# Linear attention on one core: where the middle pairs' K features lie, and who makes the last group's V blocks

## The chip, the cores and the metric

The kernel runs on one core of one Trainium2 chip. The metric is the device time of one execution in microseconds (us). A core has five engines that run their own instruction streams in order: TensorE (PE, with its weight loads PEld), VectorE (DVE), ScalarE (ACT), GpSimd (POOL) and SyncE (SP). They wait for each other by semaphores. 16 DMA engines move data between the main memory and the on-chip buffers; a transfer is issued by an engine, here by POOL (queue q0) or by SP (queue q1).

## The reference

Q, K and V have the shape 8 x 12 x 512 x 64 (batch, heads, positions, features), in float32. Features are `max(0, x) + 1`. For each of the 96 heads a 64 x 64 matrix of keys and values is made, and a sum of the K features; each query row is then multiplied with both and divided.

```python
Q_feat = np.maximum(0, Q) + 1
K_feat = np.maximum(0, K) + 1
KV = np.einsum('bhkd,bhkv->bhdv', K_feat, V)
K_sum = np.sum(K_feat, axis=2)
numerator = np.einsum('bhqd,bhdv->bhqv', Q_feat, KV)
denominator = np.einsum('bhqd,bhd->bhq', Q_feat, K_sum)
return numerator / (denominator[:, :, :, None] + 1e-10)
```

## The kernel before

The 96 heads are cut into 12 groups of 8 heads, and these into 6 pairs of groups (pair s holds groups 2s and 2s + 1). Everything is issued in an order written out by hand. `load_pair` loads V, K and Q of a pair from POOL, narrowing them to bf16 on the way, two pairs ahead. The first half of Q is loaded by SP into a tile of the pool that later holds the output (`load_first_q`).

For a group, `k_features` (VectorE, L180) makes the K features, and `v_blocks` makes four copies of V, each multiplied with one of four 0/1 masks of partitions (`v_all`). Two of the blocks are made in full by ScalarE (L213); of the other two VectorE makes all (L211): in the code `cut = 2 if b < 2 else 0`, where `cut` says how many of a block's two halves VectorE makes. `sums` (POOL, L200) puts the masks beside V, so that the same matmuls give the sum of the K features. `keys_values` (TensorE, L237, L246 or L256) adds up features times V blocks over 16 steps in PSUM; it is called in quarters. `keys_values_copies` (ScalarE, L271) copies the result to `kva_all`. `q_features` (VectorE, L180), `transposes` (TensorE, L284) and `transpose_copies` (ScalarE, L289) prepare Q. `output` makes, for each of four parts (g, h, i) of a group, the out matmuls (L302) into one of two PSUM tiles, and then `norms`: a reciprocal (L318) and a multiply (L319) on VectorE, which writes to the output tile `o_sb`. The out matmuls of the third part need the PSUM tile that the norms of the first part free. `output` takes a list `between`, whose first two entries are called after the first and the second norms.

Iteration s makes the output of pair s - 1 and the keys and values of pair s. The last one (s = 5, `end`) has an order of its own: K features and VectorE's V blocks of the last group, 11, stand at its start, ahead of `output(8)`.

K features lie in two tiles `kf_all` of 8 KB a partition. The first and the last pair (`WIDE`) use a layout with zeros beside the features, one tile for each group. The middle pairs need no zeros, and share the first tile in two halves (`kf_halves`). Before the last pair's group 11 can use that tile, POOL clears its zeros again (`clear`, L98), after iteration 4.

The pool of output tiles has five buffers (`OUT_BUFS`). Seven tiles are taken from it in turn: the first load of Q, and the outputs of pairs 0 to 5. A tile that comes to a used buffer waits for the last use of it, for an output the landing of its two stores. `store` issues a group's store: groups 0 to 9 from POOL (L164), groups 0 to 5 after iteration 3, 6 and 7 after iteration 4, 8 and 9 after iteration 5; group 10 in one and group 11 in five pieces from SP (L169 to L177).

Of the kernel before, what the change touches and what calls it, by code (L numbers as in the profile page):

```python
# [8 lines left out]
FP32 = mybir.dt.float32  # L9
BF16 = mybir.dt.bfloat16  # L10
# [9 lines left out]
def kernel(  # L20
# [16 lines left out]
    nc = tc.nc  # L37

    B, H, S, D = Q.shape
    P = 128  # L40
    C = 8
# [4 lines left out]
    NP = 4  # L46
    NG = NPAIR // NP
# [4 lines left out]
    def view(t, c):  # L52
# [15 lines left out]
    out_pool = ctx.enter_context(tc.tile_pool(name="out_pool", bufs=OUT_BUFS))  # L68
# [11 lines left out]
    kva_diag = [kva_all[:, i] for i in range(NV)]  # L80


    WIDE = (0, NG // 2 - 1)
    SHORT = NG // 2 - 2
    kf_all = [wide.tile([P, C2, 2, 2, D], BF16, name=f"kf_all_{i}") for i in range(2)]
    kf_halves = kf_all[0].rearrange("p c n h d -> p (c n h d)").rearrange(
        "p (i c n d) -> p i c n d", i=2, n=2, d=D
    )

    def kf_of(g):  # L90
        if g // 2 == 0:
            return kf_all[g]
        return kf_all[1 - g % 2] if g // 2 in WIDE else kf_halves[:, g % 2]

    def clear(t, engine):
        for h in range(2):
            zeros = t[64 - 64 * h : P - 64 * h].rearrange("p c n h d -> p (c n) h d")[:, :, h]
            engine.memset(zeros.bitcast(FP32), 0.0)  # L98
# [12 lines left out]
    def load_first_q():  # L111
        t = out_pool.tile([P, 2 * NP, C, D], FP32, name="o_sb")
        half = t[:, 0:NP].rearrange("p n c d -> p (n c) d")
        nc.sync.dma_start(out=half, in_=q_eights[:, 0])
        return half

    def load_rest_q(t):
        u = in_pool.tile([P, 2, C4, D], BF16, name="q_raw")
# [65 lines left out]
    def k_features(g):  # L184
        k_raw = raw.pop(("k", g))
        kf = kf_of(g)
        for n in range(2):
            if g // 2 in WIDE:
                for h in range(2):
                    ps = slice(64 * h, 64 * h + 64)  # L190
                    feature(kf[ps, :, n, h], k_raw[ps, n])
            else:
                feature(kf[:, :, n], k_raw[:, n])

    def mask_of(g):
        return mask_short if g // 2 == SHORT else mask
# [7 lines left out]
    def v_blocks(g, engine):  # L204
        v_raw = raw["v", g]
        mask = mask_of(g)
        for b in range(4):
            block = v_all[:, g % 2, :, :, b, 0:D]
            cut = 2 if b < 2 else 0
            if engine == "dve" and cut > 0:  # L210
                nc.vector.tensor_scalar_mul(block[:, 0:cut], v_raw[:, 0:cut], mask[:, b : b + 1])  # L211
            if engine == "act" and cut < 2:
                nc.scalar.mul(out=block[:, cut:], in_=v_raw[:, cut:], mul=mask[:, b : b + 1])  # L213
# [10 lines left out]

    def keys_values(g, lo=0, hi=C2):
        kf = kf_of(g)
        if g % 2 == 0 and lo == 0:
            kva_ps[g // 2] = [psum_kva.tile([P, BANK], FP32, name="kva_ps") for _ in range(2)]
        halves = kva_ps[g // 2]
        for c in range(lo, hi):  # L230
            for n in range(2):
                if g < 2:
                    eight, first, last_c = g, (c, n) == (0, 0), (c, n) == (C2 - 1, 1)
                else:
                    eight, first, last_c = n, g % 2 == 0 and c == 0, g % 2 == 1 and c == C2 - 1
                if g // 2 in WIDE:
                    nc.tensor.matmul(  # L237
                        halves[eight][:, 0 : 4 * DV],
                        lhsT=kf[:, c, n],
                        rhs=v_all[:, g % 2, n, c],  # L240
                        start=first,
                        stop=last_c,
                    )
                    continue
                if g // 2 == SHORT:
                    nc.tensor.matmul(  # L246
                        halves[g % 2][64 * n : 64 * n + 64, 0 : 4 * DV],
                        lhsT=kf[:, c, n],
                        rhs=v_all[:, g % 2, n, c],
                        start=c == 0,  # L250
                        stop=c == C2 - 1,
                    )
                    continue
                for h in range(2):
                    ps = slice(64 * h, 64 * h + 64)
                    nc.tensor.matmul(  # L256
                        halves[h][64 * eight : 64 * eight + 64, 0 : 4 * DV],
                        lhsT=kf[ps, c, n],
                        rhs=v_all[ps, g % 2, n, c],
                        start=first,  # L260
                        stop=last_c,
                    )
# [65 lines left out]
    def output(g, between=()):  # L328

        cells = [(g, h, i) for h in range(2) for i in range(2)]  # L330
        for k in range(4):
            if k >= 2:
                norms(*cells[k - 2])
                if k - 2 < len(between):
                    between[k - 2]()
            out_matmuls(*cells[k])
        norms(*cells[2])
        norms(*cells[3])

    def iteration(s):  # L340


        a, b = 2 * s, 2 * s + 1
        end = b == NG - 1
        quarter = C2 // 4

        def turned(g):
            transposes(g)
            transpose_copies(g)

        def first_half():
            turned(a)
            if not end:
                turned(b)
            keys_values(b, 0, quarter)

        def second_half():
            if end:
                turned(b)
            keys_values(b, quarter, 2 * quarter)  # L360

        if end:
            k_features(b)
            v_blocks(b, "dve")
        v_blocks(b, "act")
        output(a - 2, [lambda lo=lo: keys_values(a, lo, lo + quarter) for lo in (0, quarter)])
        keys_values(a, 2 * quarter, C2)
        q_features(a)
        q_features(b)
        if not end:  # L370
            k_features(b)
            v_blocks(b, "dve")
        output(a - 1, (first_half, second_half))
        keys_values(b, 2 * quarter, C2)
        if not end:
            v_blocks(a + 2, "act")
        keys_values_copies(s)
        if not end:
            k_features(a + 2)
            v_blocks(a + 2, "dve")  # L380
# [5 lines left out]

    with tc.manual_schedule():
        q_first = load_first_q()
        load("k", (0,))
        load("v", (0,))  # L390
        load_rest_q(q_first)
        load("k", (1,))
        load("v", (1,))
        for t in kf_all:
            clear(t, nc.vector)
        make_identity(nc, identity)
        nc.vector.tensor_reduce(
            out=mask,
            in_=identity.rearrange("p (h b x) -> p b h x", h=2, b=4),
            op=ALU.add,  # L400
            axis=mybir.AxisListType.XY,
        )
        nc.vector.tensor_reduce(
            out=mask_short,
            in_=identity.rearrange("p (b x) -> p b x", b=4),
            op=ALU.add,
            axis=mybir.AxisListType.X,
        )
        for i in range(2):
            t = v_all[:, i].rearrange("p n c b x -> p (n c) b x")  # L410
            nc.vector.memset(t[:, :, :, D1:], 0.0)
            sums(i, nc.vector)
        for t in kva_diag:
            for b in range(4):
                nc.gpsimd.memset(t[:, b], 0.0)
        load_pair(1)
        blocks(0)
        keys_values(0)
        q_features(0)
        q_features(1)  # L420
        transposes(0)
        blocks(1)
        transpose_copies(0)
        transposes(1)
        transpose_copies(1)
        keys_values(1)
        load_pair(2)
        keys_values_copies(0)
        blocks(2)
        for s in range(1, NG // 2):  # L430
            iteration(s)
            if s == SHORT - 1:
                sums(2 * SHORT, nc.gpsimd)
            if s + 2 < NG // 2:
                load_pair(s + 2)
            if s == SHORT - 1:
                sums(2 * SHORT + 1, nc.gpsimd)
            if s == SHORT:
                sums(2 * SHORT + 2, nc.gpsimd)
                clear(kf_all[0], nc.gpsimd)  # L440
                sums(2 * SHORT + 3, nc.gpsimd)
            for g in range(2 * s - 2, 2 * s) if s > 3 else range(2 * s) if s == 3 else ():
                store(g)
        output(NG - 2)
        output(NG - 1)
        for g in range(NG - 2, NG):
            store(g)
# [30 lines left out]
```

## Time and profile before

| | |
|---|---|
| time, median of 3 runs | 125.47 us (125.41 to 125.51) |
| the profiled execution | 125.6 us, span 123.8 us |
| granted TensorE clock, mean | 0.89 |
| DVE busy | 91.4 us (74%) |
| PE busy | 70.3 us (57%) |
| ACT busy | 69.0 us (56%) |
| POOL busy | 31.2 us (25%) |
| DMA queue q0 (POOL) | 28.84 MB, 95.1% of 16 engines' span |
| DMA queue q1 (SP) | 3.15 MB, 6.7% |

The span runs from the first to the last instruction in the profile; the execution's own time has some 1.8 us around it. Busy time of an engine is the time in which it has an instruction running. "Idle before" and the name after an arrow tell how long the engine sat without work ahead of an instruction, and what ended that. `x4` counts instructions merged into one line. A line's L number is that of the kernel before; in the changed kernel the same lines stand two to five further down.

### The profile page before, as it was taken

How to read it: one execution, taken by the hardware profiler on the slowest of the kernel's cores; microseconds unless marked ns; L12 is line 12 of the kernel's file. 1: busy time of each engine (PE TensorE's matmuls, PEld its weight loads, DVE VectorE, ACT ScalarE, POOL GpSimd, SP SyncE). 2: the span in 40 equal slices, each digit the busy share in tenths (PEclk: the TensorE clock that was granted, in tenths of full speed). 3: DMA queues.
4: the chain of work that ended last, by engine and by line, in shares of the span. 5: the costliest groups of instructions: out<-in, count | busy, mean ns of one | idle time of the engine just before them, and what ended most of it. 6: DMA issues, size and time to landing. Idle time of an engine off the chain costs nothing.

```text
span 123.8 us, 2524 instructions
## 1 busy us (share of the span) xinstructions
PE 70.3 (57%) x1056; PEld 52.6 (42%) x1056; DVE 91.4 (74%) x186; ACT 69.0 (56%) x73; POOL 31.2 (25%) x58
## 2 busy tenths in 40 slices
PE   0000099881596758676667746969214999944300
PEld 0000068661375436454455625957111578732200
DVE  5788771009179999998999969899799589449700
ACT  0006939729964999499945999179990003340000
POOL 6990000600000510024030673213912043020000
PEclk9999999999679999999999998699955589998555
DMA  3999999999999999999999999999999999999993
GB/s 98 335 213 213 213 213 214 216 216 213 214 214 216 212 214 213 217 216 213 211 209 212 215 219 212 218 212 213 216 314 417 419 419 421 417 408 418 406 406 130
DMA packets 9412, 32.15 MB, mean 260 GB/s; under 512 B 568, under 2 KB 824, under 8 KB 9272
## 3 DMA queue, kind: packets, MB, share of 16 engines
q0 software_dynamic: 8032, 28.84, 95.1%
q1 hardware_dynamic: 1368, 3.15, 6.7%
q8 instruction: 8, 0.13, 0.4%
q14 instruction: 4, 0.03, 0.1%
HBM read 37.75 MB, written 12.58 MB: 406 GB/s over the span
## 4 chain that ended last, share of the span: by engine, by line
DMA 38%; DVE 20%; PE 19%; ACT 10%; POOL 3%; issue 3%; ACTq 0%; POOLq 0%
DMA k_raw<-in_K_dram 27%; DMA v_raw<-in_V_dram 11%; PE kva_ps L237 9%; DVE o_sb L319 8%; ACT v_all L213 6%; PE qt_ps L284 5%; DVE kf_all L180 5%; DVE v_all L211 3%; PE o_ps L302 3%; ACT qt L289 3%; DVE qf L180 3%; PE kva_ps L256 2%; DVE recip L318 2%; POOL v_raw L137 1%; ACT kva_all L271 1%
## 5 line engine op out<-in xcount | busy, mean ns | idle before, releaser
L213 ACT ACTIVATE v_all<-v_raw,mask 128x2048 bf16<-128x2048 bf16 x24 | 46.6, 1994 | 2.4 <-DMA v_raw<-in_V_dram 2.1
L319 DVE TENSOR_TENSOR o_sb<-o_ps,recip 128x512 f32<-128x512 f32 x48 | 33.2, 692 | 1.6
L237 PE MATMUL kva_ps<-v_all,kf_all 128*128 128x272 bf16 x128 | 19.7, 316 | 19.3 <-ACT v_all L213 15.7
L302 PE MATMUL o_ps<-kva_all,qt 128*64 128x130 bf16 x384 | 19.8, 238 | 12.3 <-ACT kva_all L271 6.1
L289 ACT COPY qt<-qt_ps 128x512 f32<-128x512 f32 x24 | 12.9, 588 | 23.0 <-PE qt_ps L284 23.0
L237 PEld LDWEIGHTS <-kf_all 128*128 128x128 bf16 x128 | 13.6, 109 | 23.5 <-DVE v_all L211 15.7
L302 PEld LDWEIGHTS <-qt 128*64 128x64 bf16 x384 | 14.4, 118 | 20.6 <-issue 9.4
L180 DVE TENSOR_SCALAR kf_all<-k_raw 64x1024 bf16<-64x1024 bf16 (+1 forms) x32 | 14.6, 477 | 11.5 <-DMA k_raw<-in_K_dram 11.2
L256 PE MATMUL kva_ps<-v_all,kf_all 64*64 64x272 bf16 x384 | 15.5, 292 | 7.4 <-ACT v_all L213 4.1
L211 DVE TENSOR_SCALAR v_all<-v_raw,mask 128x2048 bf16<-128x2048 bf16 x24 | 17.2, 759 | 1.1 <-DMA v_raw<-in_V_dram 1.1
L318 DVE RECIPROCAL recip<-o_ps 128x8 f32<-128x8 f32 x48 | 9.6, 199 | 8.8 <-PE o_ps L302 8.7
L284 PE MATMUL qt_ps<-identity,qf 128*128 128x128 f32 x96 | 13.3, 281 | 4.4 <-DVE qf L180 2.8
L180 DVE TENSOR_SCALAR qf<-q_raw 128x1024 bf16<-128x1024 bf16 x22 | 15.1, 761 | 0.4 <-DMA q_raw<-in_Q_dram 0.4
L164 POOL DMA_DIRECT2D out_dram<-o_sb x10 | 9.6, 961 | 21.7 <-DVE o_sb L319 12.0
L256 PEld LDWEIGHTS <-kf_all 64*64 64x64 bf16 x384 | 10.4, 110 | 9.5 <-issue 5.2
L284 PEld LDWEIGHTS qt_ps<-identity,qf 128*128 128x128 f32 x96 | 10.2, 140 | 6.8 <-DVE qf L180 3.5
L271 ACT CAST kva_all<-kva_ps 64x260 bf16<-64x260 f32 x24 | 8.9, 372 | 5.6 <-PE kva_ps L237 5.3
L137 POOL DMA_DIRECT2D v_raw<-in_V_dram x4 | 2.9, 735 | 34.6 <-ACT qt L289 21.9
L246 PE MATMUL kva_ps<-v_all,kf_all 128*64 128x272 bf16 x64 | 6.3, 339 | 2.2 <-DVE v_all L211 2.2
L213 ACT ACT_TABLE_LOAD x1 | 1.3, 1283 | 10.4 <-DMA v_raw<-in_V_dram 10.4
L246 PEld LDWEIGHTS <-kf_all 128*64 128x64 bf16 x64 | 4.6, 135 | 2.6 <-DVE v_all L211 2.6
L200 POOL CAST v_all<-mask 128x128 bf16<-128x128 f32 x4 | 3.7, 916 | 7.2 <-DVE o_sb L319 6.5
(21 smaller groups left out, 24.3 us busy)
## 6 DMA issues: line engine op xcount, KB each, us to landing
out_dram<-o_sb POOLq DMA_DIRECT2D x10, 1024.0 KB, 24.0
v_raw<-in_V_dram POOLq DMA_DIRECT2D x5, 1024.0 KB, 13.6
k_raw<-in_K_dram POOLq DMA_DIRECT2D x5, 1024.0 KB, 17.8
q_raw<-in_Q_dram POOLq DMA_DIRECT2D x5, 1024.0 KB, 21.9
o_sb<-in_Q_dram SPq DMA_DIRECT2D x1, 1024.0 KB, 4.8
k_raw<-in_K_dram POOLq DMA_DIRECT2D x2, 512.0 KB, 9.5
v_raw<-in_V_dram POOLq DMA_DIRECT2D x2, 512.0 KB, 11.3
out_dram<-o_sb SPq DMA_DIRECT2D x1, 1024.0 KB, 6.9
```

The lines of the kernel that those rows point to most:

```text
L180: nc.vector.tensor_scalar(out=dst, in0=src, scalar1=1.0, scalar2=1.0, op0=ALU.add, op1=ALU.max)
L211: nc.vector.tensor_scalar_mul(block[:, 0:cut], v_raw[:, 0:cut], mask[:, b : b + 1])
L213: nc.scalar.mul(out=block[:, cut:], in_=v_raw[:, cut:], mul=mask[:, b : b + 1])
L237: nc.tensor.matmul(halves[eight][:, 0 : 4 * DV], lhsT=kf[:, c, n], rhs=v_all[:, g % 2, n, c], start=first, stop=last_c,)
L246: nc.tensor.matmul(halves[g % 2][64 * n : 64 * n + 64, 0 : 4 * DV], lhsT=kf[:, c, n], rhs=v_all[:, g % 2, n, c], start=c == 0, stop=c == C ...
L256: nc.tensor.matmul(halves[h][64 * eight : 64 * eight + 64, 0 : 4 * DV], lhsT=kf[ps, c, n], rhs=v_all[ps, g % 2, n, c], start=first, stop=l ...
L271: nc.scalar.copy(out=kva[ps, :, n, :], in_=halves[tile_][at, 0 : 4 * DV].rearrange("p (b x) -> p b x", b=4)[:, :, 0:D1],)
L284: nc.tensor.transpose(qt_ps[g][half][:, r], qf[:, r, half], identity)
L289: nc.scalar.copy(out=to[:, g % 2 * 2 + half].rearrange("p (q r) -> p q r", r=R), in_=t.rearrange("p r q -> p q r"),)
L302: nc.tensor.matmul(o_ps[64 * j : 64 * j + 64, c // 2 % 2, (c % 2) * W : (c % 2) * W + W], lhsT=qt[:, c // 2, q : q + 16, :, c % 2], rhs=kv ...
L318: nc.vector.reciprocal(out=recip, in_=cells[:, :, :, :, D:D1])
L319: nc.vector.tensor_tensor(out=outs[g // 2][:, 2 * h + g % 2 : 2 * NP : NP, 4 * i : 4 * i + 4].rearrange("p n (b c) d -> p b c n d", b=2), ...
```

## The change

Three things. The middle pairs' K features no longer lie in the first `kf_all` tile but in a tile taken from the output pool right after the first load of Q (`place_kf_halves`), so that eight tiles go through its five buffers; both `kf_all` tiles keep their zeros, and POOL's `clear` after iteration 4 is gone (the last pair's groups 10 and 11 now use the first and the second tile). In the last group ScalarE makes all four V blocks, and VectorE none. And the K features of that group are no longer made at the start of the last iteration but in `output(8)`, after its second norms, just ahead of the second quarter of group 10's keys and values.

```diff
     kf_all = [wide.tile([P, C2, 2, 2, D], BF16, name=f"kf_all_{i}") for i in range(2)]
-    kf_halves = kf_all[0].rearrange("p c n h d -> p (c n h d)").rearrange(
-        "p (i c n d) -> p i c n d", i=2, n=2, d=D
-    )
+    kf_halves = []
 
     def kf_of(g):
-        if g // 2 == 0:
-            return kf_all[g]
-        return kf_all[1 - g % 2] if g // 2 in WIDE else kf_halves[:, g % 2]
+        return kf_all[g % 2] if g // 2 in WIDE else kf_halves[0][:, g % 2]
...
+    def place_kf_halves():
+        t = out_pool.tile([P, 2 * NP, C, D], FP32, name="o_sb")
+        kf = t[:, 0:NP].rearrange("p n c d -> p (n c d)").bitcast(BF16)
+        kf_halves.append(kf.rearrange("p (i c n d) -> p i c n d", i=2, n=2, d=D))
...
-            cut = 2 if b < 2 else 0
+            cut = 2 if b < 2 and g < NG - 1 else 0
...
-        if end:
-            k_features(b)
-            v_blocks(b, "dve")
+        def second_quarter():
+            if end:
+                k_features(b)
+            keys_values(a, quarter, 2 * quarter)
+
         v_blocks(b, "act")
-        output(a - 2, [lambda lo=lo: keys_values(a, lo, lo + quarter) for lo in (0, quarter)])
+        output(a - 2, (lambda: keys_values(a, 0, quarter), second_quarter))
...
         q_first = load_first_q()
+        place_kf_halves()
...
                 sums(2 * SHORT + 2, nc.gpsimd)
-                clear(kf_all[0], nc.gpsimd)
                 sums(2 * SHORT + 3, nc.gpsimd)
```

## The prediction

> **What bounds the kernel now.** First the strip of the profile page (part 2), in 40 slices of 3.1 us.
>
> ```profile
> DMA  3999999999999999999999999999999999999993
> GB/s 98 335 213 213 213 213 214 216 216 213 214 214 216 212 214 213 217 216 213 211 209 212 215 219 212 218 212 213 216 314 417 419 419 421 417 408 418 406 406 130
> HBM read 37.75 MB, written 12.58 MB: 406 GB/s over the span
> ```
>
> The DMA engines are busy in every slice but the first and the last. Up to about 92 us they load (213 GB/s are counted on the narrowed side, twice that is read), then they store at some 415 GB/s: 12 stores of 1.05 MB, 2.5 us each. So an engine's saved time is worth nothing by itself. What counts is whether stores are issued early enough to keep the DMA engines fed to the end.
>
> Second, the last pair on VectorE (timeline of DVE), and the first two stores (out_dram's instructions from 72.0 to 73.2 us).
>
> ```profile
> 87.54 3.22 DVE L180 TENSOR_SCALAR kf_all<-k_raw 64x1024 bf16<-64x1024 bf16 x4 [0.65 <-DMA k_raw<-in_K_dram]
> 92.11 1.81 DVE L180 TENSOR_SCALAR kf_all<-k_raw 64x1024 bf16<-64x1024 bf16 x4
> 93.94 1.42 DVE L211 TENSOR_SCALAR v_all<-v_raw,mask 128x2048 bf16<-128x2048 bf16 x2
> 95.50 0.69 DVE L319 TENSOR_TENSOR o_sb<-o_ps,recip 128x512 f32<-128x512 f32 x1
> 99.44 0.21 DVE L318 RECIPROCAL recip<-o_ps 128x8 f32<-128x8 f32 x1 [1.56 <-PE o_ps L302]
> 100.29 2.62 DVE L180 TENSOR_SCALAR qf<-q_raw 128x1024 bf16<-128x1024 bf16 x4
> ...
> L164 POOL DMA_DIRECT2D out_dram<-o_sb x2: 787/830/872, 72.3 to 73.0; - x2
> DMA to landing us min/median/max: 23.2/24.0/24.9
> ```
>
> K of the last pair lands at 87.5; then VectorE has no idle time until 97.9. Its first norm of group 8 multiplies at 95.50. The stores of groups 0 and 1, issued at 72.3 and 73.0, land 23.2 and 24.9 us later, at 95.5 and 97.9, for they queue behind the last loads.
>
> Third, the tail: SP's timeline, the DMA view from 115.6 to 122.6 us, and the engine windows after it (us, PE, PEld, DVE, ACT, POOL, PEclk, DMA share, GB/s).
>
> ```profile
> 113.59 0.40 SPq L169 DMA_DIRECT2D out_dram<-o_sb  x1
> 118.67 0.46 SPq L177 DMA_DIRECT2D out_dram<-o_sb  x1
> ...
> q1 hardware_dynamic: 1224, 2.10, 78.3%
> q0 software_dynamic: 109, 0.38, 13.6%
> ...
> 121.00:122.00 1.00, 0.00 (x0) 0.00 (x0) 0.00 (x0) 0.00 (x0) 0.00 (x0) 0.50 0.80 292
> 122.00:122.60 0.60, 0.00 (x0) 0.00 (x0) 0.00 (x0) 0.00 (x0) 0.00 (x0) 0.50 0.11 38
> ```
>
> Queue q1 carries SP's stores (groups 10 and 11, 2.10 MB), q0 POOL's. SP's first store is issued at 113.59; the DMA view of 113.6 to 115.6 has no q1 packet, the next microsecond has both queues. So 2.0 us pass from issue to first bytes. At that moment q0 still holds 0.38 MB, 0.9 us of work at 410 GB/s. That is the whole cover: delay SP's stores by more than 0.9 us and the average DMA engine falls idle. Bytes end at 122.6, and 1.2 us of closing work follow.
>
> **The change, part by part.**
>
> *New place of the K features.* The middle pairs' features go to one more user of the out pool's five buffers. No instruction is added; the pool's turn moves. In the built program of the change, the output tile of pair 4 takes the buffer that pair 0's output had, so the first multiply of group 8 waits for the two semaphores of the stores of groups 0 and 1. In the kernel before, the same double wait stands at the first multiply of group 10, at 110.35, long after both landings. These stores sit in one queue behind loads that the change doesn't touch, so they still land at 95.5 and 97.9. The multiply goes from 95.50 to 97.9: **+2.4 us**. Behind it wait, on VectorE, the rest of output(8), all Q features and the last group's K features; on TensorE, the out matmuls of (8,1,0), which need a PSUM buffer that this multiply frees, and everything after them in order.
>
> *Work taken from before that multiply.* POOL's clear of `kf_all[0]` (2 MEMSETs, 2.1 us) goes. While it and POOL's neighbours ran, two of the four K feature instructions of group 10 took 1.16 and 1.17 us, against 0.42 undisturbed: 1.5 us. The four K features of group 11 (4 x 0.42 = 1.7) and its two V blocks (1.42) go too. In all 4.6 us: VectorE would reach the norm at 90.9. It then sits idle for 7 us instead; this is worth nothing.
>
> *K features of group 11 after two norms.* The 1.7 us now lie where VectorE idled 1.56 us for TensorE (the line at 99.44). Net 0.2 on VectorE, hidden from TensorE, which reaches the transposes of group 10 at 102.29, 0.7 after their Q features. Without that cover it costs 0.2.
>
> *ScalarE's V blocks.* Two more ACTIVATEs of 1.95 us: ScalarE works from 88.71 to 96.5 instead of 92.6. Group 11's first key-value matmuls start at 103.21, and will start later, so 6.7 us of cover; ScalarE idles 10.4 us there. Zero. If the V blocks slipped past that, each microsecond would count in full.
>
> *TensorE's clock.* The windows view, cut at the 3.41 us steps at which the granted clock changed:
>
> ```profile
> 93.40:96.82 3.42, 1.42 (x12) 0.67 (x10) 3.33 (x7) 0.00 (x0) 0.30 (x1) 0.50 1.02 420
> 96.82:100.23 3.41, 3.41 (x23) 2.04 (x22) 1.77 (x5) 0.00 (x0) 0.00 (x0) 0.50 1.02 420
> 100.23:103.64 3.41, 3.41 (x41) 2.85 (x40) 3.38 (x8) 0.66 (x2) 2.55 (x1) 1.00 1.03 418
> 110.47:113.88 3.41, 1.52 (x32) 1.05 (x32) 3.27 (x9) 0.00 (x0) 0.00 (x0) 1.00 1.03 418
> ```
>
> A stretch with 1.42 us of matmuls was followed by half clock, one with 3.41 by full clock (and 1.52 by half again, at 113.88). Before, TensorE runs without a gap from 96.25 and gets full speed 4.0 us later. After, it starts at 97.9 + 0.69 + 0.05 = 98.65. If full speed again comes 4.0 us on, the shift stays 2.4. Had the steps the same phase, the stretch to 100.23 would hold 1.6 us of matmuls, between the 1.52 that wasn't enough and the 3.41 that was; with half clock until 103.64, eight key-value matmuls more run at 1.93 instead of 0.93, half of which falls in the extra microsecond: +0.5, shift 2.9. The best phase is held by VectorE: norms, 1.7 of K features, two norms, 2.6 of Q features and a norm from 97.9 end the first norm of group 9 at 106.3 where it ended at 103.7, ahead of matmuls with 0.5 to spare: shift at least 2.1. The worst phase adds a microsecond to 2.4. I take 2.5 out of 2.1 to 3.4.
>
> The Trainium skill (TensorE: Matmul & The Clock Gate, Part 1) says that the activity window is 3413 ns and free-running, not tied to the kernel's start. By that rule any of these phases can come, in any run; the steps of this trace agree in length, and a single trace can't show the phase of another.
>
> *Tail.* SP's first store goes from 113.59 to 116.1. With 2.0 us to first bytes that is 118.1; q0 alone would be empty at about 116.5 on average, its slowest engines a microsecond later (the ragged 292 and 38 GB/s at the end show that spread). So all engines start q1 idle, and 2.10 MB at 410 GB/s take 5.1 us: 123.2 to 123.3 instead of 122.6, **+0.7 us**. The last store, issued at 121.2, has its first bytes 1.0 to 2.0 us on (next lines) and needs 0.5 us for its 192 KB: 122.7 to 123.7, about the same end. Bounds: the Q load that SP issues at 0.75 moves bytes from 1.8, only 1.0 us after issue. With 1.0, q1 starts at 117.1 and the bytes would be out by 122.2 but for the slow engines, so 122.6 stands, +0.0. With a shift of 3.4 and 2.0 us: +1.6. I take 2.0, since that row is this very store. The bytes and their order stay, so the tail goes below nothing only if the landing wait isn't met at all (third rival).
>
> The Trainium skill (DMA: Bandwidth & Descriptors, Anatomy of one DMA) gives about 2.0 us plus bytes over 436 GB/s per transfer on GpSimd's path. By it the last 192 KB, issued at 121.2, would land at 123.6 as an estimate, against 118.67 + 4.2 = 122.9 before: +0.7 too, by another road, and a floor under the tail even where the cover held. No row here shows an unqueued store.
>
> **Sum.** The profiled execution took 125.6 us (span 123.8): 125.6 + 0.7 = 126.3. It lies 0.13 above the median of 125.47; against that, 126.2.
>
> **The rivals.**
>
> *The half clock lasts a step longer*: shift 2.9 to 3.4, end +1.1 to +1.6, 126.6 to 127.0. For it: the 1.6 us in the doubtful stretch. Against it: with another phase of the steps it doesn't happen. Chance 0.25. The free-running window of the Trainium skill (TensorE: Matmul & The Clock Gate, Part 1) is what would let it come and go between runs.
>
> *The DMA backlog absorbs it*: no change, 125.5. It needs first bytes in 1.0 to 1.3 us after SP's issue, or a shift of 2.0 or less. For it: the Q load's 1.0, and slow engines that have work anyway until nearly 117.5. Against it: 2.0 for the store itself. Chance 0.2.
>
> *The landing wait bites nothing* and the kernel becomes faster: if groups 0 and 1 landed before VectorE came to the norm at 90.9, VectorE would be 4.6 ahead, 3 after the moved K features, and SP's stores would be queued on every engine before q0 ran dry. All bytes are then fed; at best the spread at the end, 122.6 against some 121.7 for the average engine, shrinks by half: -0.4, 125.1. The point is a landing of group 1 seven microseconds earlier, against a queue that is full. Chance 0.05.
>
> That the change doesn't do what it says can be left out: in the built program the clear is gone, and ScalarE has four V blocks.
>
> **How the numbers follow.** Forecast 0.5: +0.25 to +1.1, 126.2 as its middle. The rivals have 0.25, 0.2 and 0.05. A measurement of this kernel can tell about 0.2%, 0.25 us. Slower has the forecast and the first rival, with some 0.02 of the absorbed case above the bound: 0.77. Same 0.18, faster 0.05. The range goes from 125.4, which takes in the absorbed case, to 127.0, the end of the long half clock.
>
> **What would show it.** VectorE idle some 7 us before the first multiply of group 8, ended by out_dram's DMA at 97.9; K features of group 10 at 0.42 us each; ScalarE done with V near 96.5; SP's first store near 116.1; a dip in GB/s just before 118; last bytes near 123.3. The forecast is wrong if that multiply runs before 97, if SP's first store is issued before 115.6, or if the DMA strip has no dip and the end stays.

## The result, and the profile after

The change made the kernel slower: 127.13 us in the median of 22 runs (126.10 to 128.44) against 125.54 us for the kernel before, run beside it (22 runs, 125.27 to 127.48). The ratio is 1.0094, with a 95% interval of 1.0068 to 1.0119. On the first median of 125.47 us that ratio is +1.2 us, or 126.65; the forecast was 126.2, the range 125.4 to 127.0. The raw median lies 0.1 above that range: the medians differ by 1.6 us, the means by 1.2 (127.11 against 125.91), since the kernel before has some late runs, which raise its mean and not its median. Both kernels scatter more than three runs showed; what goes with that is looked at below. The profiled execution of the changed kernel took 127.48 us, one of its later runs, with a span of 125.7 against 123.8: 1.9 us more.

The strip of the page first. Near its end it shows what the page of before did not: a slice at 6 tenths and 261 GB/s between fuller ones.

```profile
DMA  3999999999999999999999999999999999999692
GB/s 104 325 218 211 212 214 218 214 211 218 215 211 216 211 218 211 215 218 212 209 212 211 220 214 212 214 218 214 224 390 420 421 418 416 420 418 392 261 364 87
```

On VectorE the first norm of group 8 now has its reciprocal at 91.92, and then nothing runs until its multiply. The last bracket of a line tells how long the engine idled before it and what ended that: here the stores to `out_dram`.

```profile
88.21 2.37 DVE L182 TENSOR_SCALAR kf_all<-k_raw 64x1024 bf16<-64x1024 bf16 x4
91.92 0.20 DVE L320 RECIPROCAL recip<-o_ps 128x8 f32<-128x8 f32 x1
97.75 0.69 DVE L321 TENSOR_TENSOR o_sb<-o_ps,recip 128x512 f32<-128x512 f32 x1 [5.63 <-DMA out_dram<-o_sb]
99.20 1.71 DVE L182 TENSOR_SCALAR kf_all<-k_raw 64x1024 bf16<-64x1024 bf16 x4
102.64 2.60 DVE L182 TENSOR_SCALAR qf<-q_raw 128x1024 bf16<-128x1024 bf16 x4
```

The multiply is 2.25 us later than before (95.50). ScalarE's four V blocks are made from 89.63 to 97.3, long before the matmuls that need them, at 106.43. TensorE waits for the multiply and then runs at half clock, in the windows view cut at this run's own clock steps (us, PE, PEld, DVE, ACT, POOL, PEclk, DMA share, GB/s):

```profile
94.21:97.63 3.42, 0.00 (x0) 0.00 (x0) 0.00 (x0) 3.10 (x2) 0.00 (x0) 0.50 1.02 420
97.63:101.04 3.41, 2.54 (x18) 1.49 (x20) 3.18 (x8) 0.00 (x0) 0.00 (x0) 0.50 1.02 418
101.04:104.46 3.42, 3.42 (x22) 2.30 (x22) 3.35 (x7) 0.00 (x0) 1.45 (x1) 0.50 1.02 418
```

In the kernel before full clock came at 100.23, here at 104.46. So SP's first store is 3.2 us later (116.80 against 113.59). SP's timeline of the changed kernel, and its tail in the windows view:

```profile
116.80 0.40 SPq L171 DMA_DIRECT2D out_dram<-o_sb  x1
121.43 0.37 SPq L179 DMA_DIRECT2D out_dram<-o_sb  x1
...
116.80:117.70 0.90, 0.45 (x10) 0.29 (x11) 0.86 (x3) 0.00 (x0) 0.00 (x0) 1.00 0.05 18
117.70:122.00 4.30, 1.03 (x16) 0.62 (x16) 2.33 (x6) 0.00 (x0) 0.00 (x0) 0.55 1.04 404
122.00:122.60 0.60, 0.00 (x0) 0.00 (x0) 0.00 (x0) 0.00 (x0) 0.00 (x0) 0.50 0.90 160
122.60:123.50 0.90, 0.00 (x0) 0.00 (x0) 0.00 (x0) 0.00 (x0) 0.00 (x0) 0.50 0.66 224
123.50:124.50 1.00, 0.00 (x0) 0.00 (x0) 0.00 (x0) 0.00 (x0) 0.00 (x0) 0.50 0.18 61
```

Two readings. The 0.9 us after SP's first issue move almost nothing (18 GB/s): the dip that was forecast, but the first bytes come 0.9 us after the issue, not 2.0. And the end is ragged: 160, 224, then 61 GB/s, a DMA share of 0.18, which is three engines of sixteen. The trace's record of the last store's semaphore agrees: thirteen of its sixteen parts have landed by 123.59 us, the other three at 124.67 to 124.78. From 123.0 on the data packets still to come have 512 and 1536 bytes, the sizes of the split and of the last store.

### The profile page after: what moved, and what is told of

It is laid out like the page before. It is cut to its first block, busy times and chain, and to the rows that moved or that the text cites. A ratio compares the mean times of both kernels' runs of the same rounds, so it can differ in the third digit from the quotient of the medians.

```text
span 125.7 us, 2520 instructions
## 1 busy us (share of the span) xinstructions
PE 72.9 (58%) x1056; PEld 53.7 (43%) x1056; DVE 90.6 (72%) x184; ACT 72.6 (58%) x75; POOL 30.0 (24%) x56
## 4 chain that ended last, share of the span: by engine, by line
DMA 43%; PE 23%; DVE 15%; ACT 9%; POOL 3%; issue 2%; ACTq 0%; DVEq 0%; POOLq 0%
DMA out_dram<-o_sb 19%; DMA k_raw<-in_K_dram 13%; DMA v_raw<-in_V_dram 11%; PE kva_ps L239 10%; DVE o_sb L321 7%; ACT v_all L215 6%; PE o_ps L304 5%; PE kva_ps L258 5%; PE qt_ps L286 4%; DVE qf L182 4%; DVE v_all L213 2%; ACT qt L291 2%; DVE recip L320 1%; DVE o_sb L182 1%; ACT kva_all L273 1%
## 5 line engine op out<-in xcount | busy, mean ns | idle before, releaser
L215 ACT ACTIVATE v_all<-v_raw,mask 128x2048 bf16<-128x2048 bf16 x26 | 50.4, 1994 | 2.3 <-DMA v_raw<-in_V_dram 2.1
L239 PE MATMUL kva_ps<-v_all,kf_all 128*128 128x272 bf16 x128 | 21.0, 331 | 18.2 <-ACT v_all L215 15.7
L239 PEld LDWEIGHTS <-kf_all 128*128 128x128 bf16 x128 | 14.2, 114 | 23.2 <-DVE v_all L213 14.6
L258 PE MATMUL kva_ps<-v_all,o_sb 64*64 64x272 bf16 x384 | 16.6, 307 | 7.6 <-ACT v_all L215 4.1
L213 DVE TENSOR_SCALAR v_all<-v_raw,mask 128x2048 bf16<-128x2048 bf16 x22 | 16.3, 783 | 1.2 <-DMA v_raw<-in_V_dram 1.2
L258 PEld LDWEIGHTS <-o_sb 64*64 64x64 bf16 x384 | 10.7, 116 | 10.3 <-issue 5.9
L182 DVE TENSOR_SCALAR o_sb<-k_raw 128x1024 bf16<-128x1024 bf16 x16 | 6.9, 475 | 9.0 <-DMA k_raw<-in_K_dram 8.9
L182 DVE TENSOR_SCALAR kf_all<-k_raw 64x1024 bf16<-64x1024 bf16 x16 | 7.6, 474 | 1.0 <-DMA k_raw<-in_K_dram 0.8
L248 PE MATMUL kva_ps<-v_all,o_sb 128*64 128x272 bf16 x64 | 6.3, 338 | 2.9 <-DVE v_all L213 2.9
```

The lines of the kernel that those rows point to most:

```text
L182: nc.vector.tensor_scalar(out=dst, in0=src, scalar1=1.0, scalar2=1.0, op0=ALU.add, op1=ALU.max)
L239: nc.tensor.matmul(halves[eight][:, 0 : 4 * DV], lhsT=kf[:, c, n], rhs=v_all[:, g % 2, n, c], start=first, stop=last_c,)
L258: nc.tensor.matmul(halves[h][64 * eight : 64 * eight + 64, 0 : 4 * DV], lhsT=kf[ps, c, n], rhs=v_all[ps, g % 2, n, c], start=first, stop=l ...
```

## The experiments

Each is timed against the kernel before, on the same chip and in the same rounds.

**Without the landing wait.** In the changed kernel, pair 4's output takes the K features' own tile.

```diff
         t = out_pool.tile([P, 2 * NP, C, D], FP32, name="o_sb")
+        outs[SHORT] = t
...
-        if (g % 2, h, i) == (0, 0, 0):
+        if (g % 2, h, i) == (0, 0, 0) and g // 2 != SHORT:
             outs[g // 2] = out_pool.tile([P, 2 * NP, C, D], FP32, name="o_sb")
```

> The changed kernel, but pair 4's output goes into the very tile that held the middle pairs' K features, instead of the buffer that pair 0's output left; nothing else differs. Landing-wait theory: the first multiply of group 8 no longer waits for the stores of groups 0 and 1, it runs near 92 us instead of 97.75, SP's first store is issued some 3 us earlier than in the kernel before (near 111), and the time falls back to 125.3 to 125.6 us, as before. Rival (the moved K features and ScalarE's two more V blocks cost the time): 126.5 us or more, as changed.

Measured 125.64 us, ratio 0.9974 (0.9944 to 1.0004). The multiply stands at 91.15, SP's first store at 109.12 (two lines of its timelines):

```profile
91.15 0.69 DVE L322 TENSOR_TENSOR o_sb<-o_ps,recip 128x512 f32<-128x512 f32 x1
...
109.12 0.39 SPq L172 DMA_DIRECT2D out_dram<-o_sb  x1
```

The whole loss is gone with the wait, while the moved K features and ScalarE's V blocks stay. And 4.5 us of earlier stores buy nothing clear of noise: the span is 123.9 in this profile, 123.8 before.

**The two parts of the change, each alone.** `storage_alone` is the changed kernel with these lines of before put back, `order_alone` the kernel before with them taken over:

```diff
-            cut = 2 if b < 2 and g < NG - 1 else 0
+            cut = 2 if b < 2 else 0
...
-        def second_quarter():
-            if end:
-                k_features(b)
-            keys_values(a, quarter, 2 * quarter)
+        if end:
+            k_features(b)
+            v_blocks(b, "dve")
...
-        output(a - 2, (lambda: keys_values(a, 0, quarter), second_quarter))
+        output(a - 2, [lambda lo=lo: keys_values(a, lo, lo + quarter) for lo in (0, quarter)])
```

> The storage part of the change alone: K features of the middle pairs in an output buffer and no clear, but K features and V blocks of group 11 where they were, at the start of the last iteration. Landing-wait theory: the multiply of group 8 still waits until 97.7, VectorE idles some 2.5 us before it instead of 5.6, and the time is that of the changed kernel within 0.4 us, 126.7 to 127.1 us. Rival (the moved K features and V blocks cost the time): 125.5 us, as before.

> The other part alone: the storage of before, with POOL's clear, but ScalarE makes all V blocks of group 11, whose K features follow two norms. Landing-wait theory: no wait, the first multiply of group 8 runs near 92.5 us, and the time is 125.3 to 125.6 us, as before. Rival (moved K features and V blocks cost the time): 126.5 us or more.

Storage alone: 126.98 us, ratio 1.0090 (1.0052 to 1.0128), the same loss as the whole change. Order alone: 125.90 us, ratio 0.9997 (0.9966 to 1.0028), none. The waiting multiply of storage alone in VectorE's timeline:

```profile
98.24 0.69 DVE L321 TENSOR_TENSOR o_sb<-o_ps,recip 128x512 f32<-128x512 f32 x1 [3.85 <-DMA out_dram<-o_sb]
```

**The half clock.** Transposes that nobody reads keep TensorE busy while it waits for the multiply.

```diff
+WARM = 24
...
+        def first_quarter():
+            keys_values(a, 0, quarter)
+            if end:
+                t = psum_qt.tile([P, R, P], FP32, name="qt_ps")
+                for k in range(WARM):
+                    nc.tensor.transpose(t[:, k % R], identity, identity)
...
-        output(a - 2, (lambda: keys_values(a, 0, quarter), second_quarter))
+        output(a - 2, (first_quarter, second_quarter))
```

> The changed kernel with 24 transposes of the identity, whose results nobody reads, put on TensorE between the first quarter of group 10's keys and values and the out matmuls that wait for the first multiply of group 8. They fill the 4.4 us in which TensorE idled. If the half clock after that idle time makes the shift from 2.25 us at the multiply to 3.2 us at SP's first store, the granted clock is full by 98.5, SP's first store comes at 115.7 to 116.0 instead of 116.8, and the time falls by 0.7 to 1.0 us against the changed kernel, to 126.1 to 126.4. If VectorE's chain sets the shift by itself, no change: 127.1 us.

Measured 126.46 us, ratio 1.0050 (1.0021 to 1.0079), so about 0.4% of the time is back, a little less than expected. That interval overlaps the changed kernel's (1.0068 to 1.0119), so the times alone make the gain likely and don't show it. The windows view, cut at the stretches before and after the multiply, and SP's first store:

```profile
94.40:98.50 4.10, 2.08 (x19) 1.84 (x19) 0.75 (x2) 2.64 (x2) 0.00 (x0) 0.99 1.02 420
98.50:104.50 6.00, 4.98 (x60) 3.66 (x61) 5.82 (x13) 0.00 (x0) 1.48 (x1) 1.00 1.03 419
...
115.47 0.40 SPq L172 DMA_DIRECT2D out_dram<-o_sb  x1
```

With full clock throughout, the multiply still runs at 97.75, but the shift of SP's first store falls from 3.2 to 1.9 us: part of the 2.25 us is even caught up. In these two profiles the lag that goes with the half clock is 1.3 us.

**How late may the stores be?** `late_short` and `late_long` have no landing wait, but extra VectorE work ahead of the norms of group 10, of 24 and 36 small reductions.

```diff
+        for _ in range(LATE):
+            nc.vector.tensor_reduce(
+                out=mask_row[:, 8:12],
+                in_=identity.rearrange("p (b x) -> p b x", b=4),
+                op=ALU.add,
+                axis=mybir.AxisListType.X,
+            )
         output(NG - 2)
```

> The changed kernel with pair 4's output in the tile of the K features (no landing wait), and 24 small reductions on VectorE, whose result nobody reads, ahead of the norms of group 10: about 6.7 us, of which 2.2 fill idle time. SP's first store should come near 113.6 us, as in the kernel before, and its last near 118.7. Cover theory (only the last store's issue counts, and only beyond 119.6 us, since an unqueued last store lands 3.3 us after its issue and that of before landed at 122.9): no cost, 125.5 to 125.7 us. Rival (every microsecond by which VectorE is later costs one): 4.5 us over the kernel without reductions.

> The same with 36 reductions, about 10 us: SP's first store near 117 us and its last near 121.5, as in the changed kernel, but with no landing wait and no late matmuls ahead of it. Cover theory: the end is the last store's issue + 3.3 + 0.9 us of closing work, so the span is about 125.7 and the time about 127.4 us, 1.9 us over the kernel without reductions though VectorE is some 7.7 us later. Rival (the landing wait costs by something else than SP's late issue): below 126 us.

Both delays came out too large. A reduction took 0.32 us in its chain (11.51 us for 36), not the 0.28 that the expectation had worked with. And VectorE came to the reductions 2.1 and 1.6 us later than `own_buffer` would have (the multiply ahead of them stands at 104.83 and 104.38, there at 102.76); full clock had come later too, at 97.95 and 96.67 instead of 95.33. So the short one, meant as a free delay, landed where the long one was meant, and the medians (126.20, ratio 1.0029, 0.9992 to 1.0065; and 129.68, ratio 1.0310, 1.0260 to 1.0360) miss what was expected. `late_short`'s runs spread from 125.53 to 127.71, and its profiled execution (127.23) is among the three longest. The profiles are more use than the times. Here are all that have the three last pieces, in the order of the last issue:

| profile | SP's first store | SP's last store, issued | to its landing | landed | span |
|---|---|---|---|---|---|
| own_buffer | 109.12 | 116.75 | 6.3 | 123.0 | 123.9 |
| kernel before | 113.59 | 118.67 | 4.2 | 122.9 | 123.8 |
| order_alone | 112.90 | 119.07 | 3.8 | 122.8 | 124.0 |
| warm_before (below) | 113.06 | 119.23 | 3.6 | 122.8 | 123.8 |
| warm_gap | 115.47 | 120.09 | 3.3 | 123.4 | 124.3 |
| storage_alone | 116.08 | 120.71 | 3.3 | 124.0 | 125.0 |
| late_short | 116.57 | 121.19 | 3.4 | 124.5 | 125.5 |
| changed kernel | 116.80 | 121.43 | 3.4 | 124.8 | 125.7 |
| late_long | 119.97 | 124.59 | 3.4 | 127.9 | 128.9 |

Up to some point the landing stays at 122.9, however early the issue: the bytes set it. Beyond, it is the last issue and 3.3 to 3.4 us, with 0.9 to follow. The two lines cross at an issue near 119.5, 0.8 to 0.9 us later than before; 119.23 still lies on the one and 120.09 on the other. That is the cover. `late_short` and the changed kernel, one with the landing wait and one without, lie on the same line: in these profiles the end follows from SP's late issue, whatever made it late.

The 3.3 to 3.4 us aren't the time of a store that is alone. At the last issue of the changed kernel, 121.43, SP's earlier pieces still fill the engines (404 GB/s to 122.00). What repeats is the way from SP's first bytes to the last: 6.7 us in `late_short`, the changed kernel and `late_long`, where POOL's bytes had ended by then. The next experiment shortens it.

**The three slow engines at the end.** The last 256 KB in one store.

```diff
-        cut = C - 2
-        for ps in (slice(0, 123), slice(123, P)):
-            nc.sync.dma_start(out=o_to[ps, 7, cut:], in_=o_sb[ps, 7, cut:])
-        nc.sync.dma_start(out=o_to[:, 7, 0:cut], in_=o_sb[:, 7, 0:cut])
+        nc.sync.dma_start(out=o_to[:, 7], in_=o_sb[:, 7])
```

> The changed kernel, but the last 256 KB of group 11 leave in one store over 128 partitions instead of three (123 partitions, 5 partitions, the rest). In the changed kernel 13 engines have landed the last store at 123.6, three only at 124.7: those three alone carry the piece of 123 partitions. If that piece, made for a full queue, sets the end where the queue is empty, the time falls by 0.8 to 1.2 us against the changed kernel, to about 126.0 to 126.3. If the end is set by the issue time and a fixed latency, it falls by at most 0.4 (one issue less).

Measured 125.73 us, ratio 0.9984 (0.9956 to 1.0012): the loss is gone, though the landing wait is still there, and in the profile the long half clock too (until 104.21). The profiled execution, the longest of the 12 runs (126.29), has its first SP store at 116.97, 0.2 later than in the changed kernel; its last store is issued at 120.71, lands 2.9 us later, and the bytes end evenly (its windows view):

```profile
120.00:122.00 2.00, 0.00 (x0) 0.00 (x0) 0.30 (x1) 0.00 (x0) 0.00 (x0) 0.50 1.05 406
122.00:123.20 1.20, 0.00 (x0) 0.00 (x0) 0.00 (x0) 0.00 (x0) 0.00 (x0) 0.50 0.93 357
123.20:124.50 1.30, 0.00 (x0) 0.00 (x0) 0.00 (x0) 0.00 (x0) 0.00 (x0) 0.50 0.00 0
```

Its span is 1.2 us shorter than the changed kernel's, though SP began 0.2 later: from SP's first bytes to the last, the same 2.10 MB take 5.3 us (117.90 to 123.19) instead of 6.7 (117.74 to 124.46). By the times the gain is 1.1% (1.0094 against 0.9984), 1.4 us too, somewhat above what was expected. The run takes away the uneven layout and two issues at once, so that the last issue comes 0.7 earlier. That the layout is what counts is read from the changed kernel's trace: thirteen parts of its last store landed at 123.59 in spite of the later issue, as all sixteen do here (123.58).

**Why runs of one kernel differ.** The kernel before, with transposes that nobody reads in the two gaps of TensorE around the first quarter of group 10.

```diff
+        def busy(n):
+            t = psum_qt.tile([P, R, P], FP32, name="qt_ps")
+            for k in range(n):
+                nc.tensor.transpose(t[:, k % R], identity, identity)
+
+        def first_quarter():
+            if end:
+                busy(20)
+            keys_values(a, 0, quarter)
+            if end:
+                busy(10)
+
-        output(a - 2, [lambda lo=lo: keys_values(a, lo, lo + quarter) for lo in (0, quarter)])
+        output(a - 2, (first_quarter, lambda: keys_values(a, quarter, 2 * quarter)))
```

> The kernel before with 20 and 10 transposes of the identity, whose results nobody reads, around the first quarter of group 10's keys and values, where TensorE idled 3.7 and 2.0 us. If the phase of the clock's steps is what spreads the runs of the kernel before (125.4 to 127.4), its runs now lie between 125.3 and 125.8; the profile has full clock from 92 us on and SP's first store a microsecond or so earlier. If not, the spread stays.

Median 125.52, ratio 0.9990 (0.9968 to 1.0011). Eleven of 12 runs lie between 125.39 and 125.76 and one at 126.14; of the 29 runs of the plain kernel beside it ten lie above 126, up to 126.97. SP's first store came at 113.06 instead of 113.59, half of what was expected. So most of the spread seems to go with the gaps. One profile shows how: that of `before_whole` (next), the same program up to SP's stores, has half clock until 101.91 instead of 100.23, and its first SP store at 114.44, 0.85 later. That each late run had such a phase of the clock is likely, but the phase of an unprofiled run isn't known.

**Both remedies together, and the one store in the kernel before.** The edits are those of `own_buffer` and `whole_tail`, and of `whole_tail` alone.

> Pair 4's output in the tile of the K features (no landing wait), and the last 256 KB in one store: the two remedies together, as a candidate for the fastest version. With no landing wait SP's stores are queued early and the DMA engines end when the bytes are out, so the one store should bring little beyond the first remedy: 125.3 to 125.7 us. If the split of 123, 5 and the rest evens out the engines' ends where the queue is full, one store costs up to 0.5 us: 126.1.

> The kernel before with the last 256 KB in one store instead of three. Its queue is full to the end: if the split only hurts where the queue is empty, no change or up to 0.5 us slower, 125.5 to 126.0 us in the median, but its late runs (126 to 127.4), in which SP's stores come too late, should shrink below 126.3.

Own tile and one store: 125.56 us, ratio 0.9978 (0.9951 to 1.0006), 11 of 12 runs between 125.43 and 125.66. One store in the kernel before: 125.57, ratio 0.9983 (0.9955 to 1.0010), with two runs of 12 above 126, at most 126.22. Neither beats the kernel before beyond its interval. The first has none of the late runs, of which the kernel before has six in 23 above 126 beside it, up to 126.91; for the second, two in 12 are too few to tell. Where the DMA engines were full to the end, no run here gained more.

## Why the prediction was right, and where its terms were off

*The cause* was as forecast, point by point: pair 4's output came to stand behind the stores of groups 0 and 1, whose two semaphores the multiply at 97.75 waits for in the trace; those landed at 95.2 and 97.6 (forecast 95.5 and 97.9); VectorE waited with 4.6 us of saved work in hand; ScalarE's blocks and the moved K features cost nothing. `own_buffer`, `storage_alone` and `order_alone` show it from three sides. The idle time was 5.6 us, not 7, since VectorE came to the features of group 10 0.7 us later in this run and two of them still met GpSimd: 2.37 us for four.

*The multiply's shift*: 2.4 forecast, 2.25 measured.

*The clock*: a shift of 2.5 taken from 2.1 to 3.4; the profile has 3.2, and `warm_gap` 1.9. This term was undersized, and the reason lies in the step about the doubtful stretch. The prediction held 1.6 us of matmuls in a stretch against a row with 1.52; but in that row the clock was full and fell, which says nothing on how it rises. Here 2.54 us of 3.41 still did not raise the clock. What did in the profile of before is a stretch of 3.41, and one of 3.06 at its 32nd microsecond that the prediction didn't use. Other traces bring the limit closer: 2.70 was enough in `before_whole`, 2.73 wasn't in `late_short` (each shown with the stretch that follows, whose clock stands in the column of 0.50 and 1.00):

```profile
31.96:35.38 3.42, 3.06 (x48) 1.97 (x47) 0.90 (x2) 3.42 (x3) 0.00 (x0) 0.50 1.06 212
35.38:38.79 3.41, 2.72 (x62) 2.20 (x58) 3.13 (x6) 0.88 (x2) 0.00 (x0) 1.00 1.06 214
...
74.60:78.01 3.41, 2.70 (x33) 2.23 (x35) 3.15 (x7) 3.05 (x2) 1.06 (x3) 0.50 1.06 213
78.01:81.42 3.41, 2.56 (x44) 2.28 (x40) 3.17 (x6) 0.24 (x1) 0.66 (x1) 1.00 1.06 214
...
91.13:94.54 3.41, 2.73 (x18) 1.59 (x19) 3.31 (x8) 3.41 (x3) 0.75 (x1) 0.50 1.03 395
94.54:97.95 3.41, 3.41 (x22) 2.05 (x21) 2.59 (x7) 2.63 (x2) 0.00 (x0) 0.50 1.02 419
```

So some four fifths of a stretch must be busy, and, as an estimate from these rows, TensorE without gaps gets full clock 2.7 us after its first matmul at best and 2.7 + 3.4 = 6.1 at worst: 4.0 before, 6.0 in the changed kernel. The first rival had this as its case, at 0.25; it deserved about as much as the forecast. The steps of the two profiles lie 0.8 us apart in their spans, as the free-running window of the Trainium skill (TensorE: Matmul & The Clock Gate, Part 1) would have it. Its table has full clock "After ≥1 busy SHORT window (~3.4µs sustained)"; the 2.54 that failed agrees with that, the 2.70 that sufficed shows that not all of a window has to be busy. Taken at its word it would have settled the doubtful stretch.

*Issue to first bytes*: 2.0 us forecast, 0.9 measured. This step failed. The 2.0 were read from a store that was issued into a full queue; `own_buffer`, earlier still, has 3.7. The Q load at the start, 1.0, was the row to take, for it too met a queue that was nearly empty. By itself that would have made the tail nearly free.

*The last store*: forecast to end with the rest, 0.5 us after its first bytes, 1.5 to 2.5 us after its issue. Thirteen of its parts did, 2.2 us after it; three came 1.2 us later, and the whole landed after 3.35. This step failed, for the prediction let 2.10 MB flow at 410 GB/s to the end, in 5.1 us, and had no term for the layout: 61.5 KB from 123 partitions went over three engines, behind which these engines' shares of the last store waited. As an estimate from the trace, 123 packets of 512 bytes are 41 for each of three engines, and at 0.03 us a packet 1.2 us. From first bytes to last it took 6.7 us; in `whole_tail`, without the split, 5.3. The Trainium skill (DMA: Bandwidth & Descriptors, Anatomy of one DMA), with its 2.0 us plus bytes over 436 GB/s, gave 2.45 as an estimate for GpSimd's path. No run here tests that figure, for SP's last store always had SP's earlier pieces ahead of it.

*The sum*, from the two profiles: +2.25 at the multiply, +0.96 by the clock until SP's first store, -0.45 because SP issued its pieces faster, -0.88 of cover, as the last store before took 4.23 us and now takes 3.35. That makes +1.88, the difference of the spans of these two executions, of which the second is a late one; by the ratio the cost is 1.2. The forecast had +2.4, +0.1 and a cover of 1.8. Of this cover the prediction read 0.9 from what POOL's queue still held; that the runs show 0.9 too is chance, for here the uneven end sets it.

So the landing wait and its 2.4 us were understood, and the time lies in the range, but the size was partly luck. The measured +1.2 lies just above the forecast's own +0.25 to +1.1 and in the first rival's +1.1 to +1.6, whose shift of 2.9 to 3.4 the profile has too. And the rival isn't the whole account: `storage_alone` has the forecast's shift (SP's first store at 116.08, 2.5 later) and a span 1.1 to 1.2 us longer, `whole_tail` a shift of 3.4 and no loss by the times. What the prediction had wrong is the tail. A first-byte time too long and a last store too short had opposite signs, which is why +0.7 came as near to +1.2 as it did.

Left open: how often a run meets a long half clock, and what sets the 0.9 us from SP's issue to first bytes.

## What to carry to other kernels

A tile that is put into a rotating pool moves those behind it to other buffers: before using spare room there, look in the built program at which waits appear at the later tiles, and whose landing they mean. Counting turns isn't enough: eight tiles in strict turn over five buffers would have given pair 4's output the K features' own buffer, which `own_buffer` had to force, and it got pair 0's. By what rule the pool chose isn't shown here. Where DMA is full to the end, ask not what an engine saves but how late the last store may be issued: here 0.9 us with the last store in three pieces, found from landings that the bytes set and landings that follow the issue. An uneven split of the last store that costs nothing measurable while the queue is full (0.9983 without it, in `before_whole`) becomes the slowest piece as soon as the queue runs dry.

## What the runs showed of the hardware that was not expected

- 2.54 us of matmuls in a clock stretch of 3.41 us did not bring full clock back, nor did 2.73 in `late_short`; 2.70 in `before_whole` and 3.06 did.
- From SP's issue to first bytes 0.9 us where POOL's queue was nearly drained, 2.1 in the kernel before and 3.7 in `own_buffer`, with the queue full.
- A store from 123 partitions went over three DMA engines, which worked alone for the last microsecond at 61 GB/s, and held up three of the sixteen parts of the next store by 1.1 to 1.2 us.
